# A two-layer hybrid trunk: first unit split by k-tile, first norm from the transposed input, last chunk in runs of 256 columns

## The chip, the cores and the metric

One core of a Trainium2 chip runs the whole program. The metric is device time in microseconds, the median of the runs shown. Five engines are spoken of: PE (TensorE, matmuls), ACT (ScalarE, activations), DVE (VectorE, elementwise work), POOL (GpSimd) and SP (SyncE, which issues most transfers). SBUF is the on-chip working memory, PSUM the memory into which PE accumulates. A semaphore tells one engine that another, or a transfer, is done.

## The reference, cut to what matters

There are two layers. Each norms its input, multiplies it with one wide projection, mixes in two recurrent groups, projects back, and adds a gated embedding. A last norm ends the trunk.

```python
for l in range(DEPTH):                      # 2
    hn = rms_norm(h, norm_w[l])             # h is (256 tokens, 2048)
    proj = hn @ w_in[l]                     # 2048 -> 8208 columns
    ...
    y = jnp.concatenate([y_a, y_b], axis=-1)
    h = h + y @ w_out[l]
    gate = jax.nn.sigmoid(h @ w_ple_gate[l])
    h = h + (p[l] @ w_ple_up[l]) * gate
return rms_norm(h, final_norm_w)
```

All data is float32. The norm divides each token by the root of its mean square over the 2048 features.

## The kernel before

**Units.** The weights stream through the core in 392 units, which the kernel calls steps and numbers from 0 (`make_plan`). A unit is a chunk of up to 512 output columns times two or four k-tiles of 128 input features, as a rule 512 KB. The first two chunks of a layer are done together: chunk 0 (in0dz, 272 columns) has four units of four k-tiles, chunk 1 (in0dk, 512 columns) eight of two, so in layer 0 units 0, 3, 6, 9 belong to in0dz and 1, 2, 4, 5, 7, 8, 10, 11 to in0dk. Unit 12 begins chunk 2, in0dv.

**Split products.** Weights and activations are each split into a high and a low part that PE multiplies fast, and three products are summed: high by high, high by low, low by high. For the weights, ACT writes whi from raw (L333) and DVE writes wlo = raw - whi (L335), both in `prep`. For the first layer's activations, ACT writes n0hi from xt times the norm weight (L405) and DVE n0lo (L408), both in `split`. The tokens are two halves of 128, m = 0 and 1, so a unit of two k-tiles is 12 matmuls and one of four 24; PE's order is that of the code.

**The norm's factor is applied late.** The per-token factor s0rt is not needed for the products. It scales the results when they are read out of PSUM (L474, L484, L951). The tokens' squares come from h, the input in token layout: eight ACT squares with a sum each (`Stat.add`, L434), then `Stat.cols` (L441 to L447: sum, mean, Ln and Exp on ACT for the inverse root, one Newton step on DVE). Four PSUM banks hold the chunks, so in0dv, third, takes the bank of in0dz and must wait until ACT and DVE have read that out.

**Loads.** SP issues the loads in a fixed order: after unit n, what `follow[n]` names. Three raw buffers hold units that wait for their split, three more pairs hold whi and wlo. A unit is loaded when its raw buffer is free, and split up to two units ahead of PE. xt0 to xt3 are the transposed input, h0 to h3 the same input by tokens, pr the small parameters, cs and ms constants.

**Order on the other engines.** A scheduler places the work of ACT, DVE and POOL by priority and data; each engine then runs its queue in that order and waits at the head of it. A scratch buffer in DRAM is cleared by a transfer that ACT's queue issues (L234) from a tile of zeros, which POOL makes by subtracting part of cs from itself (L233).

**The end.** The last chunk is the gate's fourth 512 columns in layer 1. The code ends with the products of token half 0, then half 1, and `finish` for each: sigmoid of the gate (L979 to L982), times up, plus h, a square with sum (`add_gated`), the token factor (`Stat.cols`), four scales of 512 columns and four stores.

Of the kernel before, what the change touches and what calls it, by code (L numbers as in the profile page):

```python
# [159 lines left out]
def trunk(ctx: ExitStack, tc: tile.TileContext, xT, x, pT, W, par, fw, cst, msk, eye, out):  # L160
# [13 lines left out]
    V, S, G = nc.vector, nc.scalar, nc.gpsimd  # L174
    WRAW = 3

    S.preload_act_table_set("natural_log_exp_and_others")
# [6 lines left out]
    def first(out, in_):  # L184
        tc.keep_in_program_order(nc.sync.dma_start(out=out, in_=in_))
# [1 line left out]

    xt = [mp.tile([128, 1024], F32, tag="et" if k < 2 else "kq", name=f"xt{k}", bufs=2) for k in range(4)]

    def x_(k):  # L190
        first(xt[k], xT[:, 4 * k:4 * k + 4, :].rearrange("p a b -> p (a b)"))

    def xtok(c):
        first(h[c], x[:, :, 512 * c:512 * c + 512])


    follow = {
        -1: lambda: (first(pr, par), x_(0)),
        0: lambda: x_(1),
        2: lambda: x_(2),  # L200
        5: lambda: x_(3),
        6: lambda: xtok(0),
        7: lambda: xtok(1),
        8: lambda: xtok(2),
        9: lambda: xtok(3),
        10: lambda: first(cs, cst),
        17: lambda: first(ms, msk),
    }

    def first_loads():  # L210
        follow[-1]()
        for n in range(3):
            load(n)
        state["loaded"] = 3

    ident, ones, SL, UI = (cs[:, 128 * j:128 * j + 128] for j in range(4))
    keep = cs[:, 512:768]
# [1 line left out]
    G.memset(epsc, EPS)  # L219
    lnhd = cp.tile([128, 1], F32, name="lnhd")  # L220
    G.memset(lnhd, float(-0.5 * np.log(128.0)))

    dr = pool("scratch", 1, space=bass.MemoryType.DRAM)
    d2 = dr.tile([66048], F32, name="d2")
# [3 lines left out]

    def clear_scratch():
        V.tensor_copy(SLr, SL)  # L230
        zero = tp.tile([128, 4, 128], F32, tag="tmp", name="zero")
        for i in range(4):
            G.tensor_tensor(zero[:, i], SL, SL, ALU.subtract)  # L233
        nc.scalar.dma_start(out=dfull(d2), in_=zero)  # L234

    def P(name, i, n=1):
        o = PAR[name][0] + i
# [173 lines left out]
    def norm_scales(l, kp):  # L411
        return [P("nw", l * KT + 2 * kp + j) for j in range(2)]

    def turn(c, name, scales):
# [8 lines left out]
            out.append(split(ps, 2 * c + half, scales(2 * c + half), name))  # L423
        return out

    class Stat:


# [5 lines left out]
            S.activation(tmp(self.name + f"sq{c}{m}"), h[c][:, m], AF.Square,  # L434
                         accum_out=self.ss[:, m, c:c + 1])

        def cols(self, ms=slice(0, 2)):

            small2 = lambda x: mp.tile([128, 2], F32, tag=x, name=self.name + x, bufs=2)[:, ms]
            r, x, t = small2("rt"), small2("rtx"), small2("rtt")  # L440
            V.tensor_reduce(x.unsqueeze(2), self.ss[:, ms], mybir.AxisListType.X, ALU.add)  # L441
            V.tensor_scalar(x, x, 1.0 / D, EPS, ALU.mult, ALU.add)
            S.activation(r, x, AF.Ln)
            S.activation(r, r, AF.Exp, scale=-0.5)
            V.tensor_tensor(t, r, r, ALU.mult)
            V.scalar_tensor_tensor(t, t, -0.5, x, ALU.mult, ALU.mult)
            V.scalar_tensor_tensor(r, t, 1.5, r, ALU.add, ALU.mult)  # L447
            return r


    def mix(tag, n, bufs, name):
# [525 lines left out]
    def add_gated(c, m, ps, up, st, l):  # L977
        t = tmp(f"pg{l}{c}{m}")
        S.activation(t, ps[m], AF.Exp, scale=-1.0)  # L979
# [4 lines left out]
        V.tensor_tensor(h[c][:, m], h[c][:, m], t, ALU.add)  # L984
        st.add(c, m)
# [10 lines left out]
    def finish(m, ps, up, st):  # L996

        add_gated(3, m, ps, up, st, DEPTH - 1)
        rt = st.cols(slice(m, m + 1))
        V.scalar_tensor_tensor(h[3][:, m], h[3][:, m], rt, fwt[1][:, 512:1024], ALU.mult, ALU.mult)  # L1000
        nc.sync.dma_start(out=out[:, m, 1536:2048], in_=h[3][:, m])
        for c in range(3):
            if c == 0:
                S.activation(h[c][:, m], h[c][:, m], AF.Copy, scale=rt)
            else:
                V.tensor_scalar(h[c][:, m], h[c][:, m], rt, None, ALU.mult)
            (nc.scalar if c == 0 else nc.sync).dma_start(out=out[:, m, 512 * c:512 * c + 512], in_=h[c][:, m])

    def pairs_ready(a, kts):
        return all(a[k // 2] is not None for k in kts)  # L1010

    st = Stat("s0")
    act = [None] * (KT // 2)
    first_loads()
    for l in range(DEPTH):
        row = Row()
        y = [None] * (KT // 2)
        mixers = {}
        for g in range(NG):
            mixers["d", g] = DN(l, g, row, y)  # L1020
            mixers["h", g] = HG(l, g, row, y)
        chunks, order = stage_plan("in", l)
        ps = {}
        for c, k4 in order:
            ch = chunks[c]
            if c not in ps:
                ps[c] = banks(f"in{l}{ch[0][0]}{ch[0][1]}")
                if ch[0][0] == "dk" and ch[0][1]:
                    spawn(mixers["d", ch[0][1]].decay())
            w = 2 if sum(n for _, n in chunk_cols(ch)) > 272 else 4  # L1030
            for q in range(0, 4, w):
                if l == 0 and c == 0:
                    for kp in (k4[0] // 2, k4[0] // 2 + 1):
                        act[kp] = split(xt[kp // 2][:, 512 * (kp % 2):512 * (kp % 2) + 512], kp, norm_scales(0, kp), "n0")
                if c == 0 and k4[0] == 12:
                    if l == 0:
                        gate_constants()
                        clear_scratch()
                        for cc in range(4):
                            for m in range(2):  # L1040
                                st.add(cc, m)
                    row.rt = st.cols()
# [4 lines left out]
            if k4[3] == KT - 1:  # L1047
                if c == 0:
                    write_gates(row, ps[c], l)
                    spawn(mixers["d", 0].decay())  # L1050
                kinds = [k for k, _ in ch]
                mx = mixers[ch[0][0][0], ch[0][1]]
                if kinds[0] in ("dk", "hf"):
                    spawn(getattr(mx, "".join(kinds))(ps[c], 0))
                else:
                    for i, k in enumerate(kinds):
                        if k != "ba":
                            spawn(getattr(mx, k)(ps[c], 256 * i))
# [24 lines left out]
        for c, k4 in order:  # L1083
            if c not in ps:
                ps[c] = banks(f"gate{l}{c}")
            for q in (0, 2):
                end = l + 1 == DEPTH and c == 3
                if k4[q + 1] == KT - (5 if end else 1):
                    up = [pm.tile([128, 512], F32, tag="m", name=f"up{l}{c}{m}") for m in range(2)]
                    run_step(up, pact)  # L1090
                if end and k4[q + 1] == KT - 5:
                    break
                while not pairs_ready(hact, k4[q:q + 2]):
                    tick()
# [46 lines left out]
```

## Time and profile before

| | us |
|---|---|
| median of three runs | 1315.84 |
| lowest, highest | 1312.15, 1317.99 |
| the profiled execution's own time | 1315.37 |
| its span, first to last instruction | 1313.6 |
| mean granted TensorE clock | 0.992 |

A row of a timeline gives start, duration, engine, line of the code, operation, output<-input, shapes and count, and in brackets how long the engine was idle before and what ended that. A row of the waits gives the waiting engine and line, what it waited for, total, count and longest. A row of the windows gives a stretch, its length, the busy time of PE, PEld, DVE, ACT and POOL with counts, the granted clock, the share of time that the transfer engines were busy, and GB/s.

### The profile page before, as it was taken

How to read it: one execution, taken by the hardware profiler on the slowest of the kernel's cores; microseconds unless marked ns; L12 is line 12 of the kernel's file. 1: busy time of each engine (PE TensorE's matmuls, PEld its weight loads, DVE VectorE, ACT ScalarE, POOL GpSimd, SP SyncE). 2: the span in 40 equal slices, each digit the busy share in tenths (PEclk: the TensorE clock that was granted, in tenths of full speed). 3: DMA queues.
4: the chain of work that ended last, by engine and by line, in shares of the span. 5: the costliest groups of instructions: out<-in, count | busy, mean ns of one | idle time of the engine just before them, and what ended most of it. 6: DMA issues, size and time to landing. Idle time of an engine off the chain costs nothing.

```text
span 1313.6 us, 18397 instructions
## 1 busy us (share of the span) xinstructions
PE 1274.0 (97%) x6592; PEld 1067.4 (81%) x6592; DVE 962.3 (73%) x1787; ACT 781.6 (59%) x1389; POOL 108.4 (8%) x88
## 2 busy tenths in 40 slices
PE   7899899999999999999999998999999999999995
PEld 6788788878888888888888887888888788888884
DVE  6689777976797766547658886788877969565475
ACT  5766656666665654447557564667666666444464
POOL 0201010010001110000002001111100002000010
PEclk9999999999999999999999998999999999999998
DMA  9555455445554455565555544544555454655563
GB/s 327 177 171 160 139 148 172 128 146 183 159 173 151 129 172 176 189 192 186 185 178 166 170 152 124 168 141 144 164 179 171 151 161 132 196 179 189 188 196 114
DMA packets 78172, 221.01 MB, mean 168 GB/s; under 512 B 15488, under 2 KB 24576, under 8 KB 78080
## 3 DMA queue, kind: packets, MB, share of 16 engines
q1 hardware_dynamic: 59408, 212.49, 50.5%
q10 hardware_dynamic: 18672, 7.34, 2.2%
q8 instruction: 52, 0.85, 0.3%
q14 instruction: 40, 0.33, 0.1%
HBM read 215.08 MB, written 4.72 MB: 167 GB/s over the span
## 4 chain that ended last, share of the span: by engine, by line
PE 71%; DVE 17%; ACT 5%; issue 3%; DMA 3%; POOL 0%; ACTq 0%; SPq 0%; DVEq 0%
PE gate L276 13%; PE out L276 12%; DVE wlo L335 5%; PE in1hf L276 5%; PE in0hf L276 5%; PE in1dv L276 5%; PE in1dk L276 5%; PE in0dv L276 4%; PE in0hi L276 4%; PE in1hi L276 3%; PE in0dk L276 3%; DMA raw<-W 2%; ACT whi L333 2%; PE up L276 2%; PE in1dz L276 1%
## 5 line engine op out<-in xcount | busy, mean ns | idle before, releaser
L335 DVE TENSOR_TENSOR wlo<-raw,whi 128x1024 fp32r<-128x1024 f32 (+2 forms) x398 | 483.9, 1219 | 249.4 <-ACT whi L333 247.6
L333 ACT ACTIVATE whi<-raw 128x1024 fp32r<-128x1024 f32 (+2 forms) x398 | 414.7, 1045 | 346.2 <-PE out L276 83.7
L276 PE MATMUL in0dk<-whi,n0hi 128*128 128x512 f32 x128 | 51.8, 405 | 2.7 <-ACT whi L333 2.7
L276 PE MATMUL in1hi<-whi,n1hi 128*128 128x512 f32 x128 | 52.9, 414 | 0.0
L276 PE MATMUL in0dk<-wlo,n0hi 128*128 128x512 f32 x128 | 50.7, 396 | 1.7 <-DVE wlo L335 1.7
L276 PE MATMUL in1dk<-whi,n1hi 128*128 128x512 f32 x128 | 51.2, 400 | 1.1 <-ACT pg L979 1.1
L276 PE MATMUL in1hi<-wlo,n1hi 128*128 128x512 f32 x128 | 51.1, 399 | 1.0 <-DVE wlo L335 0.9
L276 PE MATMUL in1hf<-whi,n1hi 128*128 128x512 f32 x128 | 52.0, 406 | 0.0
L276 PE MATMUL in0hf<-whi,n0hi 128*128 128x512 f32 x128 | 52.0, 406 | 0.0
L276 PE MATMUL in0hi<-whi,n0hi 128*128 128x512 f32 x128 | 52.0, 406 | 0.0
L276 PE MATMUL in1dk<-wlo,n1hi 128*128 128x512 f32 x128 | 50.1, 391 | 1.0 <-DVE wlo L335 0.8
L276 PE MATMUL in1hi<-whi,n1lo 128*128 128x512 f32 x128 | 50.9, 398 | 0.0
L276 PE MATMUL in0hi<-wlo,n0hi 128*128 128x512 f32 x128 | 50.1, 392 | 0.6 <-DVE wlo L335 0.5
L276 PE MATMUL in0dk<-whi,n0lo 128*128 128x512 f32 x128 | 50.6, 395 | 0.0
L276 PE MATMUL gate<-whi,g0hi 128*128 128x512 f32 x128 | 50.1, 392 | 0.0
L276 PE MATMUL in0hi<-whi,n0lo 128*128 128x512 f32 x128 | 50.0, 391 | 0.0
L276 PE MATMUL in0hf<-whi,n0lo 128*128 128x512 f32 x128 | 50.0, 391 | 0.0
L276 PE MATMUL in1hf<-whi,n1lo 128*128 128x512 f32 x128 | 50.0, 391 | 0.0
L276 PE MATMUL in0hf<-wlo,n0hi 128*128 128x512 f32 x128 | 49.9, 390 | 0.0
L276 PE MATMUL in1dk<-whi,n1lo 128*128 128x512 f32 x128 | 49.9, 390 | 0.0
L276 PE MATMUL in1hf<-wlo,n1hi 128*128 128x512 f32 x128 | 49.9, 390 | 0.0
L276 PE MATMUL gate<-whi,g1hi 128*128 128x512 f32 x128 | 49.9, 390 | 0.0
(1575 smaller groups left out, 3309.5 us busy)
## 6 DMA issues: line engine op xcount, KB each, us to landing
raw<-W SPq DMA_DIRECT2D x384, 512.0 KB, 3.5
raw<-W SPq DMA_DIRECT2D x8, 544.0 KB, 4.7
xt<-xT SPq DMA_DIRECT2D x4, 512.0 KB, 6.2
h<-x SPq DMA_DIRECT2D x4, 512.0 KB, 8.0
out_dram<-h SPq DMA_DIRECT2D x6, 256.0 KB, 3.1
fw<-fw ACTq DMA_DIRECT2D x2, 512.0 KB, 5.2
pin<-pT ACTq DMA_DIRECT2D x2, 256.0 KB, 3.1
out_dram<-h ACTq DMA_DIRECT2D x2, 256.0 KB, 2.8
```

The costliest lines, as they stand in the source:

```text
L276: return tc.keep_in_program_order(nc.tensor.matmul(*a, **k))
L333: S.activation(hi[:, sl], raw[:, sl], AF.Copy)
L335: V.tensor_tensor(lo[:, sl], raw[:, sl], hi[:, sl].bitcast(F32), ALU.subtract)
```

## The change

Four things change.

1. **The first unit.** xt0 and raw0 are loaded in two halves each, in turn. The 32 norm-weight columns of pr come alone on ACT's queue, the rest later on SP's. `first_prep` writes ACT's and DVE's pieces of unit 0 k-tile by k-tile, activations and weights in turn, instead of all activations and then all weights.
2. **The first norm.** The squares are taken from xt (eight ACT squares of 128x512, without a sum), as the k-tiles arrive; POOL adds them into one tile (seven adds); four PE products with a column of ones sum over the features and turn the result to tokens (x2s). This is asked for one unit earlier: `first_rt` and the read-out of chunk 0 (`finish_chunk(0)`) stand ahead of unit 11. h's four loads move from behind units 6 to 9 to behind units 22, 25, 28 and 31, cs from 10 to 8.
3. **The zeros** are a POOL memset at the start; the transfer that clears the scratch moves up in ACT's queue.
4. **The end.** `Finish` works on the last chunk in two runs of 256 columns, adds up the sums of the first three chunks beforehand, and `last_norm` interleaves half 0's scales with half 1's steps. Two of half 1's stores go on ACT's queue.

```diff
+        1: lambda: x_(1),
+        2: lambda: (first(pr[:, NNW:], par[:, NNW:]), x_(2)),
         5: lambda: x_(3),
-        6: lambda: xtok(0),
-        7: lambda: xtok(1),
-        8: lambda: xtok(2),
-        9: lambda: xtok(3),
-        10: lambda: first(cs, cst),
+        8: lambda: first(cs, cst),
         17: lambda: first(ms, msk),
+        22: lambda: xtok(0),
+        25: lambda: xtok(1),
+        28: lambda: xtok(2),
+        31: lambda: xtok(3),
...
+    def first_prep():
...
+        for k in range(4):
+            kp, sl, x, sc = k // 2, slice(T * (k % 2), T * (k % 2) + T), xt[0][:, T * k:T * k + T], P("nw", k)
+            wsl = slice(n * k, n * k + n)
+            S.activation(a[kp][0][:, sl], x, AF.Copy, scale=sc)
+            S.activation(w[0][:, wsl], raw[:, wsl], AF.Copy)
+            V.scalar_tensor_tensor(a[kp][1][:, sl], x, sc, a[kp][0][:, sl].bitcast(F32), ALU.mult, ALU.subtract)
+            V.tensor_tensor(w[1][:, wsl], raw[:, wsl], w[0][:, wsl].bitcast(F32), ALU.subtract)
...
+    def first_squares(kp):
+        sq = mp.tile([128, 512], F32, tag="R", name=f"x2{kp}", bufs=2) if not kp else tmp(f"x2{kp}")
+        S.activation(sq, xt[kp // 2][:, 512 * (kp % 2):512 * (kp % 2) + 512], AF.Square)
+        if kp:
+            G.tensor_tensor(first_ss[0], first_ss[0], sq, ALU.add)
...
+    def first_rt():
+        ps = pm.tile([128, 512], F32, tag="m", name="x2s")
+        for m in range(2):
+            for j in range(2):
+                PE.matmul(ps[:, m:m + 1], first_ss[0][:, 256 * j + 128 * m:256 * j + 128 * m + 128], onec,
+                          start=j == 0, stop=j == 1)
+        return rms_token(ps[:, 0:2], slice(0, 2), "s0")
...
+                if l == 0 and c == 1 and q == 2:
+                    for kp in (k4[0] // 2, k4[0] // 2 + 1):
+                        first_squares(kp)
...
+                if l == 0 and c == 1 and k4[0] == 12 and q == 2:
+                    row.rt = first_rt()
+                    finish_chunk(0)
...
+    def last_norm(half0, half1):
+        half1.gate1()
+        half0.scale(2, V, nc.sync)
+        half1.gate2()
+        half0.scale(0, S, nc.sync)
+        half1.add()
+        half0.scale(1, V, nc.sync)
+        half1.rt(between=lambda: half0.scale(3, V, nc.sync))
+        half1.scale(0, S, nc.scalar)
+        half1.scale(2, V, nc.sync)
+        half1.scale(1, S, nc.scalar)
+        half1.scale(3, V, nc.sync)
```

How the built programs differ is shown at three places. Names end in a buffer number, which the change shifts; x_212 and the like are the squares.

ACT's queue from the start of the data, before (xt_93 to xt_95 are xt0 to xt2; raw_111, 114, 116 and 143 are units 0 to 3):

```order
L405 ACTIVATE n0hi_127<-xt_93,pr 128x256 x2
L333 ACTIVATE whi_133<-raw_111 128x272 x4
L405 ACTIVATE n0hi_225<-xt_94,pr 128x256 x2
L405 ACTIVATE n0hi_231<-xt_94,pr 128x256 x2
L333 ACTIVATE whi_145<-raw_114 128x256 x4
L333 ACTIVATE whi_157<-raw_116 128x1024
L405 ACTIVATE n0hi_306<-xt_95,pr 128x256 x2
L405 ACTIVATE n0hi_312<-xt_95,pr 128x256 x2
L333 ACTIVATE whi_190<-raw_143 128x1088
```

And now (xt_92 to xt_94 are xt0 to xt2; raw_113, 118, 121 and 149 are units 0 to 3):

```order
L233 ACTIVATE n0ahi_129<-xt_92,pr 128x256 x2
L234 ACTIVATE whi_127<-raw_113 128x272 x2
L457 ACTIVATE x_212<-xt_92 128x512
L233 ACTIVATE n0ahi_131<-xt_92,pr 128x256 x2
L234 ACTIVATE whi_127<-raw_113 128x272 x2
L457 ACTIVATE x_214<-xt_92 128x512
L359 ACTIVATE whi_151<-raw_118 128x256 x4
L431 ACTIVATE n0hi_235<-xt_93,pr 128x256 x2
L431 ACTIVATE n0hi_241<-xt_93,pr 128x256 x2
L359 ACTIVATE whi_163<-raw_121 128x1024
L457 ACTIVATE x_296<-xt_93 128x512
L457 ACTIVATE x_299<-xt_93 128x512
```

Unit 0 alternates between activations and weights, and four squares stand ahead of the third input tile's split; a fifth follows behind these rows, ahead of unit 3's weights (raw_149).

ACT's queue at the first norm, before (whi_449 is unit 11; squares of h, named s0sq):

```order
L434 ACTIVATE s0sq_429,s0ss<-h_88 128x512
L434 ACTIVATE s0sq_431,s0ss<-h_88 128x512
L434 ACTIVATE s0sq_433,s0ss<-h_89 128x512
L434 ACTIVATE s0sq_435,s0ss<-h_89 128x512
L333 ACTIVATE whi_449<-raw_349 128x1024
L443 ACTIVATE s0rt<-s0rtx 128x2
L333 ACTIVATE whi_513<-raw_367 128x1024
L444 ACTIVATE s0rt<-s0rt 128x2
L333 ACTIVATE whi_531<-raw_447 128x1024
L484 ACTIVATE dn00kqet<-in0dk_0_185,s0rt 128x512
L955 ACTIVATE beta<-ba_477 128x16
L474 ACTIVATE dn00zs<-in0dz_0_119,s0rt 128x256
```

And now (whi_437 is unit 11, whi_539 unit 13):

```order
L359 ACTIVATE whi_388<-raw_332 128x1024
L359 ACTIVATE whi_437<-raw_362 128x1024
L359 ACTIVATE whi_467<-raw_386 128x1024
L359 ACTIVATE whi_539<-raw_435 128x1024
L480 ACTIVATE s0rt<-s0rtx 128x2
L481 ACTIVATE s0rt<-s0rt 128x2
L537 ACTIVATE dn00kqet<-in0dk_0_191,s0rt 128x512
L1008 ACTIVATE beta<-ba_503 128x16
L527 ACTIVATE dn00zs<-in0dz_0_125,s0rt 128x256
```

The squares are gone from this place. The two steps of the factor stand behind one weight split, and the read-outs of in0dk and in0dz behind them as before.

DVE's queue at the end, before (pg is the gate of a token half: pg_12106 of half 0, pg_12151 of half 1):

```order
L1000 SCALAR_TENSOR_TENSOR h_89<-h_89,s2rt,fw_11394 128x512
L1006 TENSOR_SCALAR h_87<-h_87,s2rt 128x512
L1006 TENSOR_SCALAR h_88<-h_88,s2rt 128x512
L983 TENSOR_TENSOR pg_12151<-up_12067,pg_12151 128x512
L984 TENSOR_TENSOR h_89<-h_89,pg_12151 128x512
L441 TENSOR_REDUCE s2rtx<-s2ss 128x1
L442 TENSOR_SCALAR s2rtx<-s2rtx 128x1
L445 TENSOR_TENSOR s2rtt<-s2rt 128x1
L446 SCALAR_TENSOR_TENSOR s2rtt<-s2rtt,s2rtx 128x1
L447 SCALAR_TENSOR_TENSOR s2rt<-s2rtt,s2rt 128x1
L1000 SCALAR_TENSOR_TENSOR h_89<-h_89,s2rt,fw_11394 128x512
L1006 TENSOR_SCALAR h_87<-h_87,s2rt 128x512
```

And now (pg_12165 is half 1; fr_12123 is half 0's factor, fr_12169 half 1's):

```order
L1091 TENSOR_SCALAR h_87<-h_87,fr_12123 128x512
L1075 TENSOR_TENSOR pg_12165<-up_12080,pg_12165 128x256 x2
L1076 TENSOR_TENSOR h_88<-h_88,pg_12165 128x256 x2
L1091 TENSOR_SCALAR h_86<-h_86,fr_12123 128x512
L1087 SCALAR_TENSOR_TENSOR h_88<-h_88,fr_12123,fw_11407 128x512
L1080 TENSOR_SCALAR fx_12168<-fs_12167,fpre_12166 128x1
L482 TENSOR_TENSOR fu_12170<-fr_12169 128x1
L483 SCALAR_TENSOR_TENSOR fu_12170<-fu_12170,fx_12168 128x1
L484 SCALAR_TENSOR_TENSOR fr_12169<-fu_12170,fr_12169 128x1
L1091 TENSOR_SCALAR h_87<-h_87,fr_12169 128x512
L1087 SCALAR_TENSOR_TENSOR h_88<-h_88,fr_12169,fw_11407 128x512
```

Half 0's scales are spread between half 1's steps, and two of them stand right ahead of half 1's sum (fx_12168).

More of the change, by code (lines that the diff above doesn't have):

```diff
@@ L201, in trunk @@
         5: lambda: x_(3),
[L202 to L206 removed]
+        8: lambda: first(cs, cst),
         17: lambda: first(ms, msk),
+        22: lambda: xtok(0),
+        25: lambda: xtok(1),
+        28: lambda: xtok(2),
+        31: lambda: xtok(3),
     }
     def first_loads():
[L211 to L212 removed]
+        tc.keep_in_program_order(nc.scalar.dma_start(out=pr[:, :NNW], in_=par[:, :NNW]))
@@ new lines, in first_loads @@
+        S.preload_act_table_set("natural_log_exp_and_others")
+        s = steps[0]
+        f = s["n"] * len(s["kts"])
+        raw = raws[0] = wr.tile([128, 1088], F32, tag="raw", name="raw0")
+        src = W[:128 * f].rearrange("(p f) -> p f", p=128)
+        for j in range(2):
+            first(xt[0][:, 512 * j:512 * j + 512], xT[:, 2 * j:2 * j + 2, :].rearrange("p a b -> p (a b)"))
+            first(raw[:, f // 2 * j:f // 2 * j + f // 2], src[:, f // 2 * j:f // 2 * j + f // 2])
+        for n in (1, 2):
@@ L213, in first_loads @@
             load(n)
         state["loaded"] = 3
+    def first_prep():
+        n = steps[0]["n"]
+        raw = raws.pop(0)
+        w = [ws.tile([128, 1088], F32R, tag=t, name=t + "0") for t in ("whi", "wlo")]
+        a = [[ap_.tile([128, 2 * T], F32R, tag=t, name=f"n0{t}{kp}") for t in ("ahi", "alo")] for kp in range(2)]
+        for k in range(4):
[5 more added lines that the diff above has]
+            V.tensor_tensor(w[1][:, wsl], raw[:, wsl], w[0][:, wsl].bitcast(F32), ALU.subtract)
+        ready[0] = [(w[0][:, n * k:n * k + n], w[1][:, n * k:n * k + n]) for k in range(4)]
+        state["prepped"] = 1
+        return [tuple(t) for t in a]
@@ L221, in trunk @@
     G.memset(lnhd, float(-0.5 * np.log(128.0)))
+    onec = cp.tile([128, 1], F32, name="onec")
+    G.memset(onec, 1.0)
+    zero = tp.tile([128, 512], F32, tag="tmp", name="zero")
+    G.memset(zero, 0.0)
     dr = pool("scratch", 1, space=bass.MemoryType.DRAM)
@@ L230, in clear_scratch @@
         V.tensor_copy(SLr, SL)
[L231 to L234, printed above, removed]
+        nc.scalar.dma_start(out=dfull(d2), in_=zero.rearrange("p (i c) -> p i c", i=4))
     def P(name, i, n=1):
@@ L435, in add, with cols @@
                          accum_out=self.ss[:, m, c:c + 1])
[L437 to L448, printed above, removed]
+        def cols(self):
+            x = mp.tile([128, 2], F32, tag="ssum", name=self.name + "sum", bufs=2)
+            V.tensor_reduce(x.unsqueeze(2), self.ss, mybir.AxisListType.X, ALU.add)
+            return rms_token(x, slice(0, 2), self.name)
     def mix(tag, n, bufs, name):
@@ L1038, in trunk @@
                         clear_scratch()
[L1039 to L1042, printed above, removed]
+                    else:
+                        row.rt = st.cols()
                 while not pairs_ready(act, k4[q:q + w]):
                     tick()
+                if l == 0 and c == 1 and k4[0] == 12 and q == 2:
+                    row.rt = first_rt()
+                    finish_chunk(0)
                 s = run_step(ps[c], act)
                 assert (s["what"], s["l"], s["c"], s["kts"]) == ("in", l, c, k4[q:q + w])
[L1047 to L1058, printed above, removed]
+            if k4[3] == KT - 1 and (l or c):
+                finish_chunk(c)
         hact = [None] * (KT // 2)
```

99 lines of the change are left out of this document (80 added, 19 removed).

## The prediction

> **What bounds the kernel now.** I read the page first (engine shares, chain), then the waits of PE, then the timelines of the three places that the diff touches: the first 20 us, 34 to 49 us, and the end.
>
> ```profile
> span 1313.6 us, 18397 instructions
> PE 1274.0 (97%) x6592; PEld 1067.4 (81%) x6592; DVE 962.3 (73%) x1787; ACT 781.6 (59%) x1389; POOL 108.4 (8%) x88
> PE 71%; DVE 17%; ACT 5%; issue 3%; DMA 3%; POOL 0%; ACTq 0%; SPq 0%; DVEq 0%
> ...
> PE in0dz L276 <- ACT whi L333: 7.3, 1, 7.3
> PE in0dk L276 <- ACT whi L333: 2.7, 1, 2.7
> ```
>
> PE is the bound nearly everywhere, and no edit removes a large matmul. What can change is time in which PE stands still: 7.3 us before the first matmul, one stall near 40 us, and the stretch after its last matmul. The sum is made against this execution's 1315.37 us (a span of 1313.6 and 1.8 around it). It lies 0.5 us under the median of the three runs, 1315.84, which spread over 5.8 us; the same sum from the median would differ by that 0.5.
>
> **The change, part by part. 1: the stall near 40 us.**
>
> ```profile
> 34.66 2.46 POOL L233 TENSOR_TENSOR zero<-cs 128x128 f32<-128x128 f32 x4 [33.73 <-DMA cs<-cst]
> 37.15 0.40 ACTq L234 DMA_DIRECT2D d<-zero  x1
> 37.60 0.63 ACT L434 ACTIVATE s0sq<-h 128x512 f32<-128x512 f32 x1 [2.17 <-POOL zero L233]
> 41.90 1.04 ACT L333 ACTIVATE whi<-raw 128x1024 fp32r<-128x1024 f32 x1
> ...
> 39.66 0.39 PE L276 MATMUL in0dk<-wlo,n0hi 128*128 128x512 f32 x1
> 39.88 0.39 PE L276 MATMUL in0dk<-whi,n0lo 128*128 128x512 f32 x1
> 42.99 0.50 PE L276 MATMUL in0dk<-whi,n0hi 128*128 128x512 f32 x1 [2.72 <-ACT whi L333]
> 48.46 0.28 PE L276 MATMUL in0dv<-whi,n0hi 128*128 128x256 f32 x1
> ...
> 44.30:48.50 4.20, 4.20 (x12) 3.29 (x13) 3.45 (x10) 2.33 (x7) 0.00 (x0) 0.59 0.76 208
> ```
>
> ACT's queue waits at the scratch-clearing DMA for a tile of zeros that POOL makes out of cs, then runs seven squares of h, and only then splits the weights of unit 11, for which PE waits. Matmuls of 512 columns start 0.227 us apart (39.66 to 39.88), so the twelve of unit 11 would have run from 40.11 to 42.83; in0dv starts at 48.46. The loss is 5.63 us: the wait, and behind it matmuls at a mean granted clock of 0.59. The change takes all of that out of ACT's queue there: the zeros come from a memset at the start, and the squares are spread over the first 25 us.
>
> What is late next is the norm factor, now asked for one unit earlier. PE runs four 128x1 products (x2s) ahead of unit 11; then in0dv needs the PSUM bank of in0dz, which ACT must empty with that factor.
>
> ```profile
> 43.89 0.19 ACT L444 ACTIVATE s0rt<-s0rt 128x2 f32<-128x2 f32 x1
> 45.32 1.22 DVE L335 TENSOR_TENSOR wlo<-raw,whi 128x1024 fp32r<-128x1024 f32 x1
> 46.65 0.16 DVE L447 SCALAR_TENSOR_TENSOR s0rt<-s0rtt,s0rt 128x2 f32<-128x2 f32 x1
> 46.90 0.69 ACT L484 ACTIVATE dn00kqet<-in0dk,s0rt 128x512 f32<-128x512 f32 x1 [1.87 <-DVE s0rt L447]
> 47.59 0.47 ACT L474 ACTIVATE dn00zs<-in0dz,s0rt 128x256 f32<-128x256 f32 x1
> 51.50 0.44 PE dn00pkc L279 x4
> ```
>
> In the new order a weight split of 1.04 stands ahead of the two small ACT steps (0.19 each), one wlo of 1.22 ahead of the last three DVE steps (0.2 each with their hand-over): 1.04 + 0.4, the wlo running from 1.04 to 2.26 beside them, + 0.6, makes about 2.6 us after x2s, hand-overs among it. From the factor to the end of the first dn00zs is 1.25 (46.81 to 48.06; kqet stays ahead of it). So the bank is free some 3.85 us after x2s, unit 11 takes 2.72, and PE waits 1.1. (Bounds: 0, if the scheduler's one wlo slips behind; 2.0, if a second 1-us piece gets in.) The x2s products are taken at the 0.44 of four pkc products (0.1 to 1.0). POOL's sums end long before: seven adds after a last square near 24 us, for use near 40. Term: 5.63 - 0.44 - 1.1 = **4.1 us gained** (2.6 to 5.5).
>
> **2: the first unit.** PE can start when half of xt0 and half of raw0 are there.
>
> ```profile
> 0.80 1.28 ACT L177 ACT_TABLE_LOAD   x1 [0.80 <-PEq L1133]
> 3.05 0.23 ACT L252 ACTIVATE negA<-pr 128x32 f32<-128x32 f32 x1 [0.97 <-DMA pr<-par]
> 5.03 1.70 ACT L405 ACTIVATE n0hi<-xt,pr 128x256 fp32r<-128x256 f32 x4 [1.21 <-DMA xt<-xT]
> 6.80 1.39 ACT L333 ACTIVATE whi<-raw 128x272 fp32r<-128x272 f32 x4
> 9.71 2.27 ACT L333 ACTIVATE whi<-raw 128x256 fp32r<-128x256 f32 x5
> 13.77 1.12 ACT L333 ACTIVATE whi<-raw 128x1088 fp32r<-128x1088 f32 x1 [0.17 <-DMA raw<-W]
> 14.92 1.29 DVE L335 TENSOR_TENSOR wlo<-raw,whi 128x1088 fp32r<-128x1088 f32 x1
> 17.53 0.30 PE L276 MATMUL in0dz<-wlo,n0hi 128*128 128x272 f32 x1
> L477 POOL TENSOR_TENSOR dn02sz<-dn02zs,dn02sz x1: 1285/1285/1285, 272.6 to 272.6; 128x512 f32<-128x512 f32 x1
> GB/s 327 177 171 160 139 148 172 128 146 183 159 173 151 129 172 176 189 192 186 185 178 166 170 152 124 168 141 144 164 179 171 151 161 132 196 179 189 188 196 114
> ```
>
> 154 KB (pr) had landed at 3.05 and 512 KB more at 5.03. Now 16 KB and half of xt0, 272 KB, come first: by that rate at 3.5. ACT is free by then: two DMA issues (0.40, as that of d<-zero) and the table load of 1.28 from 0.80 on end at 2.9, and the memset that the second issue waits for, which the trace lacks, can hardly cost more than POOL's 1.29 for two inputs of that size (dn02sz). What queues behind that issue is n0ahi, so a memset of more than 1.9 us would delay the start one for one. Half of raw0 follows, and PE starts near 5.0, two us earlier. But does that reach unit 3? It was ready at 16.21 (14.92 + 1.29) and used at 17.53, so there were only 1.3 us in hand. Until unit 3 is split ACT now has, from 3.5 on: twelve activation pieces (3 x 1.70), the weights of units 0 to 2 (1.39 + 2.27), five squares (at most 0.61 each, 37.60 to 41.90 for seven, accumulator read included: 3.05), negA 0.23, and unit 3 itself 1.12: 13.2 us, to 16.7. DVE adds 1.29: ready at 18.0, against 17.53 when PE needed it before. With squares 0.1 shorter and data at 3.05, 17.1. So ACT, with the squares put between, eats the early start: I take **0.3 us lost** by unit 3 (0.6 gained to 1.5 lost, which holds one POOL collision of part 4, or the 0.8 us that 256 KB of zeros take from the first loads at the 327 GB/s of the page's first slice). After it 2 us are in hand again, and the h loads no longer sit between the weights. pr's remainder, cs and the lambda constants are needed at the gates only, after 46 us; were they late, the gates would wait by their own 1 us.
>
> The four h loads go behind units 22 to 31.
>
> ```profile
> 58.16 1.06 ACT L333 ACTIVATE whi<-raw 128x1024 fp32r<-128x1024 f32 x1 [1.82 <-PE in0dv L276]
> ```
>
> There the splits wait for PE, not for weights, and 140 to 180 GB/s move where 327 did in the first slice. I cost them at nothing; with that cover gone, 0.5 MB at 327 GB/s is 1.6 us each, 6.4 in all.
>
> **3: the end.**
>
> ```profile
> 1299.60 0.39 PE L276 MATMUL gate<-whi,g1lo 128*128 128x512 f32 x1
> 1299.82 0.63 ACT L434 ACTIVATE s2sq<-h 128x512 f32<-128x512 f32 x1 [1.48 <-DVE h L984]
> 1300.44 0.58 ACT L979 ACTIVATE pg<-gate 128x512 f32<-128x512 f32 x1
> 1307.09 0.75 DVE L1000 SCALAR_TENSOR_TENSOR h<-h,s2rt,fw 128x512 f32<-128x512 f32 x1
> 1307.76 0.88 DVE L1006 TENSOR_SCALAR h<-h,s2rt 128x512 f32<-128x512 f32 x2
> 1307.87 0.33 SPq L1001 DMA_DIRECT2D out_dram<-h  x1
> ```
>
> From the last matmul's start: exp at 0.84 (half 0's square stands before it), scaling at 7.49, first store 8.27, end 14.0. Redone with runs of 256 (ACT at most 0.47 a piece, as dn00zs, the next starting 0.1 before the end; DVE 0.4, an estimate from 0.88 for two pieces of 512): half 0's squares end earlier, exp at 0.47; Ln from 1.4, the two exps end at 2.8, products and adds at 4.2 (half 0's 0.44 scale between), squares at 4.8. Then DVE first finishes two scales of half 0 (0.44 + 0.75) until 5.4, a 0.5 us delay that the new order makes; the factor takes 1.2 more, and scaling starts at 6.6. The 0.44 scale now goes ahead of the 0.75 one: first store 7.05. The stores themselves (first issue to end, 5.73) stay: end at 12.8. Term: **1.2 us gained** (0.5 to 1.8).
>
> Sum: -4.1 + 0.3 - 1.2 = -5.0, so 1310.4 us.
>
> **4: the shared port, a rule against the change.**
>
> ```profile
> 63.44 1.04 POOL L525 TENSOR_TENSOR dn01ug<-cs,gp 128x512 fp32r<-128x512 f32 x1 [8.87 <-DVE dn00kq L559]
> 63.77 1.80 DVE L335 TENSOR_TENSOR wlo<-raw,whi 128x1024 fp32r<-128x1024 f32 x1
> ```
>
> A wlo that starts during a POOL operation takes 1.80 instead of 1.22: it ends 1.09 after POOL's end at 64.48. The Trainium skill, page "SBUF — State Buffer", section "Who interferes with whom", says that whichever of the two issues first keeps the shared port for the whole instruction, a DVE instruction with two SBUF inputs among them; this row agrees. The seven adds (1.29 each, as dn02sz) fall between 8 and 26 us, where DVE makes wlo and n0lo, all with two SBUF inputs.
>
> **Rivals.**
>
> (B) The early start survives (squares overlapped, weights landing sooner) or the bank wait does not appear: 2 us from part 2, or 1.1 from part 1 with a good tail. For it: PE does start 2 us earlier. Against: ACT's sum above. Both: 1310.4 - 3.2 = 1307.2.
>
> (C) The clock.
>
> ```profile
> 795.54:802.37 6.83, 6.00 (x16) 4.89 (x17) 3.56 (x12) 2.17 (x8) 0.00 (x0) 0.50 0.24 77
> ```
>
> In layer 1, after stalls that layer 0 has too, the clock was 0.50 for 6.83 us. Nearly half of the 6.0 us that PE was busy there is what that cost: about 2.7 us, an estimate. Layer 0 did not pay. The Trainium skill, "TensorE: Matmul & The Clock Gate", section "What's actually happening", has windows of 3.4 us that run freely; 6.83 is two of them. A shifted program can pay twice, 1313.1, or not at all, 1307.7.
>
> (D) Slower: the adds of part 4 hold DVE. If each of the seven puts its 1.29 before a wlo that PE waits for, 9.0 us, less the 1.3 in hand: 1310.4 + 7.7 = 1318.1. It decides from the first add that pushes unit 2's or 3's wlo past PE's need. Against: four of the adds come where 2 us are in hand.
>
> **Chances.** Forecast 0.43, B 0.27, C 0.12 each way, D 0.06. 0.5% of 1315.84 is 6.6 us, about what a measurement here tells from no change: the bounds are 1309.3 and 1322.4. Faster: a third of the forecast, nearly all of B and of C's good side, 0.14 + 0.25 + 0.11 = 0.50. Slower: the worst of D with the runs' spread, 0.05. Same: 0.45. The forecast's own range is 1308 to 1313; with B and C, 1306 to 1315.
>
> **What would show it.** No PE wait on whi near 40 us and clock 1.00 there; in0dv near 44.3, after a wait of about 1 us for ACT's dn00zs; first matmul near 5 us, but unit 3's wlo matmul still near 17.5 to 18; last matmul to end about 12.8. I am wrong if unit 3 runs 1.5 us sooner, if PE waits on wlo that overlaps POOL's adds, or if a stall appears near the h loads.

## The result and the profile after

| | us |
|---|---|
| kernel before, median of 20 runs | 1314.66 (1312.01 to 1318.38) |
| changed kernel, median of 20 runs | 1317.72 (1314.43 to 1322.08) |
| ratio, 95% interval | 1.0021 (1.0011 to 1.0031) |
| the profiled execution of the changed kernel | 1318.54, a span of 1316.8 |

The change costs 2.8 us (1.4 to 4.1): 0.0021 of 1314.66. 1310.4 was forecast. From the page of the changed kernel, and from the waits of its PE (engine and line, what it waited for, total, count, longest):

```profile
span 1316.8 us, 18440 instructions
PE 1277.9 (97%) x6600; PEld 1068.8 (81%) x6600; DVE 966.2 (73%) x1793; ACT 782.0 (59%) x1392; POOL 119.2 (9%) x93
PE 72%; DVE 17%; ACT 5%; issue 3%; DMA 3%; ACTq 0%; SPq 0%; DVEq 0%
...
PE in0dz L302 <- ACT whi L234: 5.9, 1, 5.9
PE in0dz L302 <- DVE wlo L361: 3.1, 1, 3.1
PE in0dk L302 <- DVE wlo L361: 2.6, 1, 2.6
```

The wait of 2.7 us for ACT's whi near 40 us is gone, as forecast. Two waits for DVE's wlo are new. The shares of the page say nothing of them: 97% PE busy, as before. Lines moved with the diff: L276 is now L302, L333 is L359, L335 is L361.

**The first new wait, near 20 us.** The timelines of DVE, POOL and PE there:

```profile
13.27 2.33 DVE L361 TENSOR_TENSOR wlo<-raw,whi 128x1024 fp32r<-128x1024 f32 x1
15.53 1.27 DVE L279 TENSOR_SCALAR negA<-negA 128x32 f32<-128x32 f32 x1
16.72 3.71 DVE L434 SCALAR_TENSOR_TENSOR n0lo<-xt,pr,n0hi 128x256 fp32r<-128x256 f32 x4
20.35 2.41 DVE L361 TENSOR_TENSOR wlo<-raw,whi 128x1088 fp32r<-128x1088 f32 x2
...
13.22 6.53 POOL L459 TENSOR_TENSOR x<-x,x 128x512 f32<-128x512 f32 x4 [3.09 <-ACT x L457]
...
18.28 0.28 PE L302 MATMUL in0dz<-whi,n0hi 128*128 128x272 f32 x1
21.68 0.39 PE L302 MATMUL in0dz<-wlo,n0hi 128*128 128x272 f32 x1 [3.12 <-DVE wlo L361]
```

For 6.53 us POOL does four adds back to back, and DVE gets through only where one ends. Before, the same work stood there without POOL:

```profile
12.02 1.23 DVE L335 TENSOR_TENSOR wlo<-raw,whi 128x1024 fp32r<-128x1024 f32 x1 [0.33 <-ACT whi L333]
13.16 1.67 DVE L408 SCALAR_TENSOR_TENSOR n0lo<-xt,pr,n0hi 128x256 fp32r<-128x256 f32 x4
14.92 1.29 DVE L335 TENSOR_TENSOR wlo<-raw,whi 128x1088 fp32r<-128x1088 f32 x1
```

A wlo takes 2.33 instead of 1.23 us, four n0lo 3.71 instead of 1.67, and even negA, 32 columns, 1.27. Unit 3's wlo begins at 20.35, where it began at 14.92. That is the shared port of part 4 of the prediction; the rule quoted there from the Trainium skill ("SBUF — State Buffer", "Who interferes with whom") holds here.

**The second, near 105 us.** The queues of SP and ACT, DVE, and PE:

```profile
80.95 0.55 SPq L184 DMA_DIRECT2D h<-x  x1
...
81.44 0.33 ACTq L682 DMA_DIRECT2D dn00fx<-dn00d  x1
...
87.16 0.15 DVE L694 TENSOR_TENSOR dn00pr<-dn00fx 32x1 f32<-32x1 f32 x1 [1.73 <-DMA dn00fx<-dn00d]
106.68 1.21 DVE L361 TENSOR_TENSOR wlo<-raw,whi 128x1024 fp32r<-128x1024 f32 x1
...
104.89 0.47 PE L302 MATMUL in0dk<-whi,n0hi 128*128 128x512 f32 x1
107.94 0.50 PE L302 MATMUL in0dk<-wlo,n0hi 128*128 128x512 f32 x1 [2.58 <-DVE wlo L361]
```

DVE and PE at the same place before:

```profile
83.83 0.14 DVE L641 TENSOR_TENSOR dn00pr<-dn00fx 32x1 f32<-32x1 f32 x1
103.36 1.21 DVE L335 TENSOR_TENSOR wlo<-raw,whi 128x1024 fp32r<-128x1024 f32 x1
...
103.32 0.48 PE L276 MATMUL in0dk<-whi,n0hi 128*128 128x512 f32 x1
104.62 0.50 PE L276 MATMUL in0dk<-wlo,n0hi 128*128 128x512 f32 x1 [0.82 <-DVE wlo L335]
```

One of the moved loads of h (512 KB, SP's queue) is issued 0.5 us ahead of a small transfer on ACT's queue, the read of dn00fx back from DRAM. The list of DMA issues (KB each, us from issue to landing) has that read at 5.7 us in the changed kernel and 3.1 before:

```profile
dn00fx<-dn00d ACTq DMA_DIRECT2D x1, 32.0 KB, 5.7
...
dn00fx<-dn00d ACTq DMA_DIRECT2D x1, 32.0 KB, 3.1
```

A chain of thirty small DVE steps (dn00pr, dn00fx) hangs on that read, and unit 29's wlo stands behind it on DVE, 19.5 us after the chain's first step in both kernels (87.16 to 106.68, before 83.83 to 103.36). What comes later is the start of the chain. PE loses 2.83 us (104.89 to 107.94, less the 0.23 from one matmul's start to the next), where it lost 1.08 before.

Both waits also pay in the clock. The busy time of each engine by stretch, PE first, then the mean granted clock:

```profile
19.57:22.98 3.41, 1.30 (x10) 1.30 (x11) 3.41 (x6) 3.23 (x6) 0.18 (x1) 1.00 0.26 55
22.98:26.39 3.41, 3.41 (x16) 3.38 (x16) 3.41 (x5) 0.13 (x1) 2.06 (x1) 0.50 0.80 271
104.90:108.31 3.41, 0.83 (x6) 0.47 (x5) 3.41 (x5) 1.52 (x4) 1.61 (x2) 1.00 0.42 138
108.31:111.72 3.41, 3.41 (x10) 2.63 (x9) 3.41 (x7) 2.80 (x4) 0.00 (x0) 0.50 0.66 173
...
26.40:49.70 23.30, 23.30 (x128) 20.09 (x126) 12.17 (x24) 9.99 (x14) 1.89 (x1) 1.00 0.67 207
```

After each, 3.41 us run at half speed, some 1.7 us lost. The last row is the place of the old stall: PE is busy throughout at full clock.

### The profile page after: what moved, and what is told of

Read it like the earlier page. It is cut to its first block, busy times and chain, and to the rows that moved or that the text cites. A ratio compares the mean times of both kernels' runs of the same rounds, so it can differ in the third digit from the quotient of the medians.

```text
span 1316.8 us, 18440 instructions
## 1 busy us (share of the span) xinstructions
PE 1277.9 (97%) x6600; PEld 1068.8 (81%) x6600; DVE 966.2 (73%) x1793; ACT 782.0 (59%) x1392; POOL 119.2 (9%) x93
## 4 chain that ended last, share of the span: by engine, by line
PE 72%; DVE 17%; ACT 5%; issue 3%; DMA 3%; ACTq 0%; SPq 0%; DVEq 0%
PE gate L302 13%; PE out L302 12%; PE in1dv L302 6%; DVE wlo L361 6%; PE in1hf L302 5%; PE in1dk L302 5%; PE in0dv L302 4%; PE in0hf L302 4%; PE in0dk L302 4%; PE in1hi L302 3%; PE in0hi L302 3%; PE up L302 2%; DMA raw<-W 2%; ACT whi L359 2%; PE in0dz L302 1%
## 5 line engine op out<-in xcount | busy, mean ns | idle before, releaser
L361 DVE TENSOR_TENSOR wlo<-raw,whi 128x1024 fp32r<-128x1024 f32 (+1 forms) x394 | 484.6, 1232 | 249.1 <-ACT whi L359 247.2
L359 ACT ACTIVATE whi<-raw 128x1024 fp32r<-128x1024 f32 (+1 forms) x394 | 413.2, 1051 | 353.0 <-PE out L302 82.9
L302 PE MATMUL in1dk<-whi,n1hi 128*128 128x512 f32 x128 | 51.2, 400 | 1.1 <-ACT pg L1032 1.1
L302 PE MATMUL in1hf<-whi,n1hi 128*128 128x512 f32 x128 | 52.2, 407 | 0.0
L302 PE MATMUL in1hi<-whi,n1hi 128*128 128x512 f32 x128 | 52.0, 406 | 0.0
L302 PE MATMUL in1hi<-wlo,n1hi 128*128 128x512 f32 x128 | 50.2, 392 | 1.3 <-DVE wlo L361 1.3
L302 PE MATMUL in1dk<-wlo,n1hi 128*128 128x512 f32 x128 | 50.1, 392 | 0.9 <-DVE wlo L361 0.8
L302 PE MATMUL gate<-whi,g0hi 128*128 128x512 f32 x128 | 50.1, 392 | 0.0
L302 PE MATMUL in1hf<-whi,n1lo 128*128 128x512 f32 x128 | 50.1, 391 | 0.0
L302 PE MATMUL in1hi<-whi,n1lo 128*128 128x512 f32 x128 | 50.1, 391 | 0.0
L302 PE MATMUL in1dk<-whi,n1lo 128*128 128x512 f32 x128 | 49.9, 390 | 0.0
L302 PE MATMUL in1hf<-wlo,n1hi 128*128 128x512 f32 x128 | 49.9, 390 | 0.0
L302 PE MATMUL gate<-whi,g1hi 128*128 128x512 f32 x128 | 49.9, 390 | 0.0
L302 PE MATMUL gate<-whi,g0lo 128*128 128x512 f32 x128 | 49.8, 389 | 0.0
L302 PE MATMUL gate<-wlo,g0hi 128*128 128x512 f32 x128 | 49.8, 389 | 0.0
L302 PE MATMUL gate<-whi,g1lo 128*128 128x512 f32 x128 | 49.8, 389 | 0.0
L302 PE MATMUL gate<-wlo,g1hi 128*128 128x512 f32 x128 | 49.8, 389 | 0.0
L302 PE MATMUL in1dv<-whi,n1hi 128*128 128x512 f32 (+1 forms) x128 | 48.7, 380 | 0.0
L302 PE MATMUL in1dv<-whi,n1lo 128*128 128x512 f32 (+1 forms) x128 | 46.6, 364 | 0.0
L302 PE MATMUL in1dv<-wlo,n1hi 128*128 128x512 f32 (+1 forms) x128 | 46.5, 363 | 0.0
L302 PE MATMUL in0dk<-wlo,n0hi 128*128 128x512 f32 x96 | 38.2, 398 | 2.7 <-DVE wlo L361 2.6
L302 PE MATMUL in0dk<-whi,n0hi 128*128 128x512 f32 x96 | 39.3, 409 | 0.0
```

What stands on the lines that cost most here:

```text
L302: return tc.keep_in_program_order(nc.tensor.matmul(*a, **k))
L359: S.activation(hi[:, sl], raw[:, sl], AF.Copy)
L361: V.tensor_tensor(lo[:, sl], raw[:, sl], hi[:, sl].bitcast(F32), ALU.subtract)
```

## The experiments

Theory: two causes, GpSimd's adds (L) and the one load of h (H). Rivals: the split first unit is itself slow; the later gates delay the DN chain; the h loads slow the weights; chance in the clock windows. All ratios are to the kernel before, run beside on the same chip, with 95% intervals; 0.001 is 1.3 us. Below, a bare number names a row of this table.

| | edit | median us | ratio |
|---|---|---|---|
| 1 | changed kernel, adds on VectorE | 1314.19 | 1.0004 (0.9996 to 1.0013) |
| 2 | changed kernel, h behind units 13 to 16 | 1314.44 | 1.0004 (0.9994 to 1.0014) |
| 3 | both | 1310.17 | 0.9974 (0.9963 to 0.9984) |
| 4 | before, new end alone | 1311.69 | 0.9986 (0.9976 to 0.9996) |
| 5 | 3, old first unit | 1310.46 | 0.9972 (0.9962 to 0.9982) |
| 6 | 3, squares spread, adds on GpSimd | 1309.40 | 0.9963 (0.9950 to 0.9977) |
| 7 | 3, squares spread, adds on VectorE | 1310.17 | 0.9972 (0.9961 to 0.9984) |
| 8 | 1, one load of h moved | 1309.79 | 0.9965 (0.9953 to 0.9978) |
| 9 | 1, that load one unit later | 1310.77 | 0.9974 (0.9964 to 0.9984) |
| 10 | 7, old first unit | 1310.62 | 0.9970 (0.9960 to 0.9980) |
| 11 | before, new norm alone | 1312.25 | 0.9990 (0.9981 to 0.9999) |
| 12 | 7 again | 1309.49 | 0.9961 (0.9948 to 0.9974) |

### 1 to 3: each cause alone, and both

```diff
-            G.tensor_tensor(first_ss[0], first_ss[0], sq, ALU.add)
+            V.tensor_tensor(first_ss[0], first_ss[0], sq, ALU.add)
```

> The seven adds of the squares are on VectorE instead of GpSimd; all else is the changed kernel. Theory L (GpSimd's adds hold VectorE): VectorE's n0lo and wlo go back to 0.42 and 1.2 to 1.3 us each near 13 to 21 us; the wait for unit 3's wlo near 18 us shrinks from 3.28 us to below 1 us (VectorE now carries the adds at about 0.67 each) and the half-speed window at 23 us goes; gain 3 to 5 us on the changed kernel, ratio to the kernel before 0.998 to 1.000. Rival S (the split first unit is what is slow): the wait near 18 us stays above 2 us, ratio 1.001 to 1.003. Both leave the wait near 105 us (2.83 us) in place.

```diff
-        22: lambda: xtok(0),
-        25: lambda: xtok(1),
-        28: lambda: xtok(2),
-        31: lambda: xtok(3),
+        13: lambda: xtok(0),
+        14: lambda: xtok(1),
+        15: lambda: xtok(2),
+        16: lambda: xtok(3),
```

> The four loads of h stand behind units 13 to 16 instead of 22, 25, 28 and 31; all else is the changed kernel. Theory H (a 512 KB load issued just ahead of the round trip of dn00fx through DRAM delays it): the read of dn00fx near 81 us lands after 3.1 us instead of 5.7, the chain of dn00pr on VectorE starts 2 us earlier against TensorE, the wait for unit 29's wlo near 105 us falls from 2.83 to about 1.1 us and the half-speed window at 108 us goes; gain 2.5 to 3.5 us, ratio 0.999 to 1.000. Rival G (the chain is late because the gates are written later, behind unit 11): dn00pr starts no earlier against TensorE, the wait stays above 2.3 us, ratio 1.0015 to 1.003. Rival X: the loads of units 14 to 18 land later by 2 us or more each and TensorE waits for whi there.

> The edits of the last two kernels together. If L and H are two causes with places of their own, their gains add: 6 to 8.5 us on the changed kernel, 1309 to 1312 us, ratio 0.9955 to 0.9980. If one is a consequence of the other, or the early time is given back at a later wait, the ratio is that of the better one alone, 0.998 to 1.000.

DVE and PE in the first:

```profile
13.02 1.22 DVE L361 TENSOR_TENSOR wlo<-raw,whi 128x1024 fp32r<-128x1024 f32 x1
14.15 0.68 DVE L459 TENSOR_TENSOR x<-x,x 128x512 f32<-128x512 f32 x1
...
17.54 1.28 DVE L361 TENSOR_TENSOR wlo<-raw,whi 128x1088 fp32r<-128x1088 f32 x1
...
18.88 0.39 PE L302 MATMUL in0dz<-wlo,n0hi 128*128 128x272 f32 x1 [1.00 <-DVE wlo L361]
```

Of the same seven adds, 0.68 each on DVE, three stand ahead of unit 3's wlo, in place of 6.53 us of mutual blocking: the wait falls from 3.12 to 1.00 (a little above the "below 1" expected), the half-speed window goes, 2.2 us come back (1.0021 to 1.0004). The wait near 100 us stayed, 2.4. In the second the read takes 3.0 us and the loss at 105 us is 1.03; also 2.2 us come back, and the early wait stays. Together 6.2 us: two causes with places of their own. Each of these differences has an interval of about 1.8 us either way. Alone, each gave less than expected (3 to 5 and 2.5 to 3.5 us), and 6.2 is above 2.2 + 2.2; the intervals allow that much. The rivals of the split unit, the later gates and the slowed weights fall here: the early wait shrinks with the unit still split, dn00pr starts 1.5 us earlier (85.67) with the gates where they were, and PE waits for no whi.

### 8 and 9: which load of h, and why

```diff
-        25: lambda: xtok(1),
+        14: lambda: xtok(1),          # experiment 9: 26
```

> The changed kernel with the adds on VectorE (the first experiment) and one load of h alone moved: the second, from behind unit 25 to behind unit 14. Theory H (that load lies ahead of the round trip of dn00fx): this one load does all, the read of dn00fx lands after 3.1 us instead of 5.3, the wait near 100 us is about 1.1 us instead of 2.6, ratio 0.997 to 0.998 as with all four moved. Rival: the four loads take from the raw loads around them together, and one in four gives a quarter of the gain, ratio 0.9995 or above.

> The first experiment's kernel (adds on VectorE) with the second load of h behind unit 26 instead of 25, so that it is issued some 1.5 us after the read of dn00fx instead of 0.4 us ahead of it, while that read is still under way. Theory H in its narrow form (what is queued ahead of the small read delays it): the read lands after 3.0 to 3.6 us, the wait near 100 us is 1.0 to 1.3 us, ratio 0.9960 to 0.9980. Rival (the two transfers share the engines whichever is first): the read takes 4.3 us or more, the wait near 100 us stays above 2 us, ratio 0.999 to 1.0005.

One load does it all: 5.1 us (1.0004 to 0.9965) in 8 and 3.9 in 9, where all four give 3.9 (1 against 3); PE's wait near 100 us is 0.91 in both, instead of 2.38. In 9 the load is issued one unit later, after the small read and before that has landed. Queues of SP and ACT, and the list of issues, in 9:

```profile
78.76 0.55 SPq L184 DMA_DIRECT2D h<-x  x1
...
76.94 0.33 ACTq L682 DMA_DIRECT2D dn00fx<-dn00d  x1
...
dn00fx<-dn00d ACTq DMA_DIRECT2D x1, 32.0 KB, 3.2
```

So it matters that the load is issued shortly ahead of the read. In 9 the two did not move at the same time, though their times from issue to landing overlap: by the packet records of the traces, the read's packets (64 bytes each) moved from 78.71 to 79.56 us and those of h (2048 bytes) from 81.02 on. In 1, where the read is late, it was 79.35 to 81.68 for the read and 78.86 to 81.52 for h. Experiment 9 therefore does not test its rival, that two transfers which do move together slow each other whichever was issued first. In 8, a 512 KB weight load is issued 0.9 us ahead (76.12 against 77.00) and the read still takes 3.1; in the changed kernel a weight load and the load of h, 0.9 and 0.5 us ahead, make it 5.7. Whether the 0.5 us, the two loads together or the smaller packets of the load of h do that is not separated.

### 6, 7 and 12: the same work, spread

```diff
-                if l == 0 and c == 1 and q == 2:
-                    for kp in (k4[0] // 2, k4[0] // 2 + 1):
-                        first_squares(kp)
+                if l == 0 and c <= 1 and 0 <= state["next"] - 3 < 8:
+                    first_squares(state["next"] - 3)
```

In addition the squares, the adds and the whi and wlo of the first 13 units are kept in the order of the code, so that the scheduler can't pull the adds forward.

> The third experiment's kernel with the squares and their adds spread over the units 3 to 10 in a kept order, behind whi and wlo of unit 2, 5, 6, 8, 9, 11, and the adds on GpSimd again, where VectorE has 1.2 to 1.8 us of idle time between two wlo. Theory L (it is the overlap with VectorE's needed work that costs, not GpSimd as such): no wait above 0.6 us on wlo before 45 us, ratio 0.996 to 0.998. Rival: adds of 1.3 us or more on GpSimd hold wlo anywhere, and TensorE waits 1 us or more somewhere between 20 and 45 us, ratio 0.998 to 1.000.

> The same spread, adds on VectorE. All theories: no wait above 0.6 us before 45 us, ratio 0.996 to 0.9975; if GpSimd's adds still hold VectorE in the kernel with them spread, this one is faster by 1 us or more, otherwise the two agree within 0.5 us.

> The seventh experiment's kernel once more, beside the two kernels that it is compared with: ratio 0.9962 to 0.9982; the term of the first unit is its difference to the tenth, that of end and first unit together its difference to the eleventh (the end measured at 1.8 us by itself).

With the adds on GpSimd again (6), by stretch and from the timelines of POOL and DVE:

```profile
13.00:44.50 31.50, 31.29 (x174) 27.20 (x172) 22.37 (x37) 20.05 (x33) 12.51 (x7) 1.00 0.79 253
...
28.61 1.75 POOL L460 TENSOR_TENSOR x<-x,x 128x512 f32<-128x512 f32 x1 [0.82 <-ACT x L458]
...
33.74 2.22 DVE L362 TENSOR_TENSOR wlo<-raw,whi 128x1024 fp32r<-128x1024 f32 x1 [1.38 <-ACT whi L360]
```

PE is busy for 31.29 of 31.50 us although POOL's adds stand in 12.51 of them. Most now come behind a wlo that has begun, and it is POOL that is held (1.75 instead of the 1.28 of an add by itself). Where DVE is held, as in the wlo at 33.74 (2.22 instead of 1.23), PE does not need the result yet. So it is not the engine that costs but when its operations meet DVE's. 6 and 7 do not differ by what can be told.

### 5 and 10: the split first unit undone

> The third experiment's kernel (adds on VectorE, h behind units 13 to 16) with the first unit as in the kernel before: whole loads of pr, x and unit 0, one split after the other. Theory from the prediction: the split k-tile by k-tile loses 0.3 us by unit 3, so without it 0.3 us are gained, ratio 0.9965 to 0.9977 against 0.9974 with it; unit 3's first matmul near 17.4 to 18.4 us. Rival: the split is worth the 1 to 2 us by which the first matmul starts earlier, ratio 0.998 to 0.999.

> The seventh experiment's kernel (squares spread, adds on VectorE, h behind units 13 to 16) with the first unit as in the kernel before. With no add ahead of unit 3's wlo the early start has nothing in its way: if the split is worth its 1 to 2 us of earlier start, this kernel is slower than the next one by 1 us or more and in0dv starts 1 us later; if the early start is spent at half clock, as the in0dv times of the fifth experiment suggest, the two agree within 0.6 us.

Without the split PE's first matmul is at 8.2 to 8.3 us in these two profiles (7.28 in that of the kernel before), with it at 6.2 to 6.5. By the start of in0dv two microseconds have become -0.2 (3 against 5: 45.28 and 45.12), 0.6 (12 against 10) or 0.9 (7 against 10: 44.53). The rows of 12 and 10:

```profile
44.86 0.39 PE L302 MATMUL in0dv<-whi,n0ahi 128*128 128x256 f32 x1
...
45.42 0.39 PE L279 MATMUL in0dv<-whi,n0hi 128*128 128x256 f32 x1
```

In time neither pair can be told apart. The first matmuls run at half clock, until 10.3 to 13.5 us in the profiles of either kind.

### 4 and 11: the end and the norm alone

> The kernel before with the new end of the last chunk alone (Finish and last_norm). Theory: from the start of the last matmul to the end 12.0 us instead of 14.0, nothing else moves: ratio 0.9985 (0.9978 to 0.9992). Rival: the runs of 256 columns and the order of the half 0 stores cost as much on ScalarE as they save, ratio 0.9995 to 1.0005.

> The kernel before with the new norm alone: zeros by memset, squares from the transposed input spread over the units 3 to 10, adds on VectorE, sums on TensorE; first unit, places of the h loads and the end as before. The prediction's first term says 4.1 us (2.6 to 5.5), ratio 0.9969 (0.9958 to 0.9980), in0dv near 44.5 after a start of the first matmul near 7.3. Rival: from the difference between the third and the fourth experiment, 1.6 us, ratio 0.9988 (0.998 to 0.9995).

The end alone gives 1.8 us (0.5 to 3.2). The norm alone gives 1.3 (0.1 to 2.5), though in0dv starts at 45.16 instead of 48.46 in its profile:

```profile
45.16 0.39 PE L279 MATMUL in0dv<-whi,n0hi 128*128 128x256 f32 x1
```

That is near the rival's 1.6 and not the 4.1 of the prediction's term. Where the other 2 us go I have not shown. In that profile they are not lost on the way: layer 1's first matmul (in1dz) stands at 653.12 instead of 656.34. But that execution was itself 2.4 us below its median (1309.85 against 1312.25), so part of the lead may be chance.

## Why the prediction was wrong, point by point

- **The sign: part 4 and rival D.** The step that failed is D's "Against: four of the adds come where 2 us are in hand". It took four of the seven to come behind unit 3. Only two did (23.05 and 28.04 in POOL's timeline). ACT made four squares between 12.46 and 17.36, and their adds ran back to back from 13.22 to 19.75, against unit 2's wlo and the n0lo ahead of unit 3's wlo, where by part 2 only 1.3 us were in hand. The mechanism, its place ("unit 2's or 3's wlo") and the sign it would give were named, with a chance of 0.06; its price of 7.7 us counted all seven adds, and measured it is 2.2 us alone, 3.9 with H cured (3 against 2).
- **The h loads, "I cost them at nothing".** Wrong, by 2.2 us (changed kernel against 2) to 5.1 (1 against 8). The cover that was named, that "the splits wait for PE, not for weights", held: no whi waits there. The step asked only who waits for the loads that follow on SP's queue. The victim was on another queue, a 32 KB read with a serial chain behind it. Of "what would make me wrong" both signs came, PE waiting on a wlo that overlaps POOL's adds and a stall near the h loads.
- **Term 1, 4.1 us.** The mechanism is right: no wait near 40 us, clock 1.00 there. The size is off: at in0dv 3.3 us in 11 (3.2 against the profile of 4), in time 1.3. The 5.63 that it starts from was one execution's, in which the clock fell behind the stall. In the profile of 4, whose code is the same up to here, it did not fall (1.00 from 41.5 to 48.3):

```profile
41.87 0.39 PE L276 MATMUL in0dk<-whi,n0lo 128*128 128x512 f32 x1
43.67 0.49 PE L276 MATMUL in0dk<-whi,n0hi 128*128 128x512 f32 x1 [1.42 <-ACT whi L333]
48.32 0.39 PE L276 MATMUL in0dv<-whi,n0hi 128*128 128x256 f32 x1 [0.58 <-ACT dn00kqet L491]
```

Counted as in the prediction, in0dv could have started at 44.82 there, so the loss is 3.50, and the term's sum would give 2.0 instead of 4.1. The wait for PSUM forecast at 1.1 is 0.14 in the changed kernel and 0.28 in 11: from the end of x2s to the factor it took 2.0 us (46.89 to 48.91), not 2.6, and PE was released by dn00kqet, not by dn00zs. in0dv starts while dn00zs still reads in0dz, so by this trace it does not take the bank of in0dz, as the description of the kernel and the prediction have it, but one that dn00kqet empties. ACT and PE around it, in the changed kernel:

```profile
49.01 0.69 ACT L537 ACTIVATE dn00kqet<-in0dk,s0rt 128x512 f32<-128x512 f32 x1 [1.46 <-DVE s0rt L484]
49.70 0.47 ACT L527 ACTIVATE dn00zs<-in0dz,s0rt 128x256 f32<-128x256 f32 x1
...
49.38 0.39 PE L302 MATMUL in0dk<-whi,n0lo 128*128 128x512 f32 x1
49.75 0.39 PE L302 MATMUL in0dv<-whi,n0ahi 128*128 128x256 f32 x1
```

- **Term 2, 0.3 us lost.** Not told from nothing in time (5, 10), as forecast: the early start does not reach unit 3. The first matmul came at 5.92, not near 5.0: the small load of norm weights, issued first, was the last that ACT waited for. ACT and PE at the start:

```profile
4.48 0.91 ACT L233 ACTIVATE n0ahi<-xt,pr 128x256 fp32r<-128x256 f32 x2 [1.95 <-DMA pr<-par]
...
5.92 0.59 PE L302 MATMUL in0dz<-whi,n0ahi 128*128 128x272 f32 x1 [5.92 <-ACT whi L234]
```

- **Term 3, 1.2 us.** Right in mechanism, larger: 2.0 us in the trace (from the last matmul at 1304.79 to the end at 1316.8, 12.0 instead of 14.0), 1.8 in time. The first scale begins 6.3 us after that matmul (6.6 forecast), and first store to end takes 5.2 instead of the 5.73 that "stay": with two of half 1's stores on ACT's queue instead of one, the last issue ends 1.2 us after the first began (1311.59 to 1312.78), where it took 1.7 before (1307.87 to 1309.57). PE's last row, and DVE and the queues behind it:

```profile
1304.79 0.39 PE L302 MATMUL gate<-whi,g1lo 128*128 128x512 f32 x1
...
1311.08 0.49 DVE L1091 TENSOR_SCALAR h<-h,fr 128x512 f32<-128x512 f32 x1
...
1311.59 0.99 SPq L1092 DMA_DIRECT2D out_dram<-h  x2
...
1311.82 0.96 ACTq L1092 DMA_DIRECT2D out_dram<-h  x2
```

- **The sum.** The gains measured alone are 1.8 (end) and 1.3 (norm), 3.1 us. The two causes take 6.2 (changed kernel against 3): 3.1 slower by that sum, 2.8 measured. With both causes cured the ratios of 0.9961 to 0.9974 are near the forecast's 0.9962 (1310.4 over 1315.37).
- **Rivals B and C.** The bank wait did not appear, as B has it, but the early start did not survive (B's two terms make 3.1, not 3.2). Of C: the clock did fall in different places. Between the first matmuls and the last it was at half for 10.2 us in the profile before (at 44.6 and 795.5) and for 6.8 in that of the changed kernel. But chance alone does not make the result, since the interval of the ratio excludes 1, and 1 to 3 move the time with the two places.

## What to carry to other kernels

An operation put on an idle engine is not free where it shares a port with a busy one: find which of the busy engine's operations it will meet, in the order the scheduler really makes, and hold the sum of the two against the slack of the next result that is waited for. A transfer moved to a quiet place is to be held against every transfer issued just after it, on any queue; the victim is the small read that a serial chain waits for, not the bulk stream beside it. A stall that is taken out, and an engine that starts sooner, are worth only what reaches the next place where something else is late.

## What the runs showed of the hardware

- **Most of the spread between runs goes with the granted clock.** Over the 195 runs of these kernels whose clock is on record, taken about each group's mean, the time falls by 1.0 us for each 0.001 of mean granted clock, and with that taken out the spread (standard deviation) falls from 1.42 to 0.84 us. At equal clock (0.994) by that line the changed kernel would stand at 1316.8, the first experiment at 1313.0, the second at 1313.3, the third at 1310.7, the kernel before at 1313.1 to 1313.4. That makes the two causes 3.7 and 3.5 us alone and 6.1 together, where the measured ratios make them 2.2, 2.2 and 6.2.
- **Two idle microseconds are enough.** In the windows above PE was busy for 1.30 and 0.83 of 3.41 us, and the next 3.41 ran at half clock. The Trainium skill, "TensorE: Matmul & The Clock Gate", "What's actually happening", has windows of 3.4 us that run freely, which agrees, and the drop after at least one idle window; here windows a quarter and more than a third busy were enough. The fourteen profiles, cut into such stretches from the first step to full clock on, bear this out: every stretch at full clock with PE busy for 1.67 us or less was followed by one at half clock, and none with 2.1 us or more was.
